# The first token tile in two halves, zero products on TensorE meanwhile, other banks for the first projections, and an earlier sum in the last stage

## The chip, the cores and the metric

The kernel runs on one core of a Trainium2 chip. The metric is the device time of one execution in microseconds (us), lower is better; the time before is the median of three runs. The engines are TensorE (PE, with its weight loads as PEld), VectorE (DVE), ScalarE (ACT), GpSimd (POOL) and SyncE (SP, which here only issues transfers). Each engine works through its own queue in order, and semaphores join the queues.

## What is computed

One decoder layer on 512 tokens of width 1024, with 16 learned meta tokens put ahead of them (so 528 positions). What matters here is the beginning and the end:

```python
h = jnp.concatenate([meta, x], axis=1)
mix = hybrid_mixer(rmsnorm(h, norm_mix_pre[l]), w_in[l], ...)   # proj = hn @ w_in, split into rq rk rv rg sq sk sv ga gb
h = h + rmsnorm(mix, norm_mix_post[l])
ff = swiglu(rmsnorm(h, norm_ffn_pre[l]), w_ffn_in[l], w_ffn_out[l])
h = h + rmsnorm(ff, norm_ffn_post[l])
return h[:, N_META:]
```

where `rmsnorm(x, g) = x * rsqrt(mean(x*x) + 1e-6) * g`. The first part of the mixer that the kernel computes is the stick-breaking attention: 16 heads of width 64 from the columns sq, sk, sv of `w_in`.

## The kernel before

All matrix products are made in three: each operand is split into a high part (rounded to the product's format, by ACT) and a low part (the rest, by DVE), and high×high, high×low and low×high are added up in one bank. The helper `split` (line 98) does this; its ACT half is line 99 and its DVE half line 96 (`lo_of`). So every weight and every activation passes ACT and DVE once before TensorE can use it.

The tile framework orders the instructions of each engine: it takes them by a simulated timeline, with program order as priority, and allots the buffers of each pool. An instruction marked `keep_in_program_order` stays behind what was traced before it on its engine.

**The first stage** (lines 701 to 763) prepares the tokens and the first attention operands:

- The gain vector `norm_mix_pre` is loaded as `grow` (8 x 128), turned by TensorE, copied to `gcol` by ACT, and spread over all partitions by eight transposes into `gps`, which takes a double bank of PSUM from `bank_a`.
- `xload(i)` loads token tile i (128 tokens x 1024, 512 KB) into a part of `ysb` that is free at this time; tile 4 is the 16 meta tokens.
- `innorm(i)` takes the sum of squares on ACT (line 719, with its output thrown into a double bank `junk`), scales it on DVE, takes the power -0.5 on POOL (`rstd_of`, lines 142 and 143), multiplies the tile with it and with `gps` on DVE (`hx`, two instructions of 512 columns, line 724), transposes it in eight steps on TensorE (line 93) and splits it into `hT` and `hL`.
- `Values(c)` is a block of 256 columns of sv: 1 MB of weights, loaded by `load_units` into one of two `raw` buffers and split into two units of four row blocks each; there are five buffers for units. `part((j,))` makes 24 products of 256 columns for token tile j in a bank of `bank_p` (two single banks), and its result is split into `vt`. `tail` does the same for the meta tokens, 16 products of 256 columns.
- `qk_work(work, 0)` adds the projections q and k of the first pair of heads to a work list, which is drained after all of `Values`: q is 24 products of 512 columns in a bank of `bank_p`, k is two times 24 products of 264 columns in one bank each. Each bank is emptied by ACT (lines 506 to 526) and DVE (line 96).

Then the eight pairs of heads follow. In each, TensorE's order is fixed by hand (`pinned[0]`): the pair's scores (in `bank_a`), transposes and value products alternate with the projections of the next pair (in `bank_p`). The first piece of pair 0 is a stretch of projection q of pair 1 with no score in it; then come the scores.

**The last stage** (lines 1252 to 1268) finishes the second FFN product by token tiles. For each half c of a tile's 1024 columns, ACT takes the sum of squares of the bank (line 1260) and DVE multiplies the bank with the gain (line 1261). Then DVE adds both sums (line 1263), POOL takes the power -0.5 (line 1264), DVE scales and adds the residual (line 1267) and SP stores each half.

Of the kernel before, what the change touches and what calls it, by code (L numbers as in the profile page):

```python
# [10 lines left out]
F32 = mybir.dt.float32  # L11
F32R = mybir.dt.float32r
# [4 lines left out]
P = 128  # L17
# [17 lines left out]
def hybrid_block(  # L35
# [65 lines left out]
            tc.keep_in_program_order(ins)  # L101
        lo_of(lo, src, hi)

    def load_units(src, kn, cn, views, wun=wun):

        raw = wraw.tile([P, kn, cn], F32, tag="raw", name="raw")
        nc.sync.dma_start(raw, src.rearrange("(k p) c -> p k c", p=P))
        res = []
        for ks, kl, cs, cl in views:
            wh = wun.tile([P, kl, cl], F32R, tag="wh", name="wh")  # L110
            wl = wun.tile([P, kl, cl], F32R, tag="wl", name="wl")
            split(wh, wl, raw[:, ks : ks + kl, cs : cs + cl])
            res.append((wh, wl))
        return res
# [293 lines left out]
    with tc.tile_pool(name="s2", bufs=2, side=RS, reuse_waits="tile") as s2:  # L408
# [28 lines left out]
        class Values:  # L437
# [2 lines left out]
            def __init__(self, c):  # L440
                self.c = c

            def load(self):
                c = self.c
                src = w_in[:, O_SV + 256 * c : O_SV + 256 * (c + 1)]
                self.vt = vts[c] = s2.tile([P, NT, 4, P], F32R, tag="vt", name="vt")
                self.units = load_units(src, KD, 256, [(0, 4, 0, 256), (4, 4, 0, 256)])

            def part(self, js):
                vt = self.vt  # L450
# [43 lines left out]
        qks = {}  # L494
        flat = lambda t: t.rearrange("p a b -> p (a b)")

        def qk_work(work, p):
            def q_load():
                return feat_units(w_in[:, O_SQ + P * p : O_SQ + P * (p + 1)])

            def q_steps(us):
                ps = bank_p()
                yield from feat_steps(ps, us[0], xtok, ltok)
                qa = s2.tile([P, T], F32R, tag="qa", name="qa", bufs=1)
                qb = s2.tile([P, T], F32R, tag="qb", name="qb")
                nc.scalar.activation(qa[0:64], ps[0:64], AF.Copy)
                nc.scalar.activation(qb[64:128], ps[64:128], AF.Copy)
                lo_of(qa[64:128], ps[0:64], qa[0:64])
                lo_of(qb[0:64], ps[64:128], qb[64:128])
                qks[p] = [(qa, qb)]  # L510

            def k_load():
                return feat_units(w_in[:, O_SK + P * p : O_SK + P * (p + 1)])

            def k_steps(us):
                ka = s2.tile([P, 2, 264], F32R, tag="ka", name="ka", bufs=1)
                kb = s2.tile([P, 2, 264], F32R, tag="kb", name="kb")
                kl1 = kl1s[p % 2]
                for i in range(2):
                    cs = slice(264 * i, 264 * (i + 1))  # L520
                    pk = bank_p()[:, :264]
                    yield from feat_steps(pk, us[0], lambda k: hT[:, k, cs], lambda k: hL[:, k, cs])
                    nc.scalar.activation(ka[0:64, i], pk[0:64], AF.Copy)
                    nc.scalar.activation(ka[64:128, i], pk[0:64], AF.Copy)
                    nc.scalar.activation(kb[64:128, i], pk[64:128], AF.Copy)
                    nc.scalar.activation(kb[0:64, i], pk[64:128], AF.Copy)
                    lo_of(kl0[0:64, i], pk[0:64], ka[0:64, i])
                    lo_of(kl1[64:128, i], pk[64:128], kb[64:128, i])
                qks[p] += [(flat(ka), flat(kb)), (flat(kl0), flat(kl1))]

            work.add(q_load, q_steps)
            work.add(k_load, k_steps)

# [169 lines left out]
        xts = [ysb[:, 2 * i : 2 * i + 2, :].rearrange("p a b -> p (a b)") for i in range(NT)]  # L703
        xts.append(xts[0])
        gps = bank_a()

        def xload(i):
            if i == NT:
                nc.sync.dma_start(xts[i][:NM], meta)
            else:  # L710
                nc.sync.dma_start(xts[i], x[i * P : (i + 1) * P, :])

        def innorm(i):
# [2 lines left out]
            xt = xts[i]  # L716
            junk = bank_a().rearrange("p a b -> p (a b)")
            ss = cst.tile([P, 1], F32, name=f"ss{i}")
            nc.scalar.activation(junk[:n], xt[:n], AF.Square, accum_out=ss[:n])
            rstd_of(ss[:n], ss[:n], 1e-6, 1.0 / D, n)  # L720
            for j in range(2):
                hx = s2.tile([P, 512], F32, tag="qb", name="hx")
                cs = slice(512 * j, 512 * (j + 1))
# [4 lines left out]
                ks = slice(4 * j, 4 * j + 4)  # L728
                split(hT[:, ks, c0 : c0 + n], hL[:, ks, c0 : c0 + n], pt[:, :, :n])

        nc.sync.dma_start(grow, g_mix_pre.rearrange("o (k p) -> (o k) p", p=P))
        xload(0)

        pg = bank_b()
        turned(pg[:, :KD], grow, ident[:KD, :KD])
        nc.scalar.activation(gcol, pg[:, :KD], AF.Copy)
        for k in range(KD):
            turned(gps[:, k // 4, (k % 4) * P : (k % 4 + 1) * P], gcol[:, k : k + 1].to_broadcast([P, P]), ident)
        vals = [Values(0), Values(1)]
        innorm(0)  # L740
        vals[0].load()
        xload(1)
        vals[1].load()
        innorm(1)
        for i in range(2, NT + 1):
            xload(i)
        work = Work()
        qk_work(work, 0)
        for j in range(NT):
            for v in vals:  # L750
                for _ in v.part((j,)):
# [462 lines left out]
    with tc.tile_pool(name="s8", bufs=2, side=RS, reuse_waits="tile") as s8:  # L1214
# [38 lines left out]
        for i in range(NT):  # L1253
            sc, fo = [col("sc0"), col("sc1")], s8.tile([P, D], F32, tag="fo", name="fo")
            for c in range(2):
# [2 lines left out]
                cs = slice(512 * c, 512 * (c + 1))  # L1258
                sq = s8.tile([P, 512], F32, tag="sq", name="sq")
                nc.scalar.activation(sq, banks[i][c], AF.Square, scale=D**-0.5, accum_out=sc[c])  # L1260
                nc.vector.tensor_tensor(fo[:, cs], banks[i][c], gfin[:, cs], op=ALU.mult)
            rs = col("rs")
            nc.vector.scalar_tensor_tensor(rs, sc[0], 1e-6, sc[1], op0=ALU.add, op1=ALU.add)
            nc.gpsimd.tensor_tensor(rs, rs, nhalf, op=ALU.pow)
            for c in range(2):
                cs = slice(512 * c, 512 * (c + 1))
                nc.vector.scalar_tensor_tensor(fo[:, cs], fo[:, cs], rs, h2[:, i, cs], op0=ALU.mult, op1=ALU.add)
# [44 lines left out]
```

## Time and profile before

| | |
|---|---|
| median of 3 runs | 1215.48 us (1213.07 to 1216.57) |
| the profiled execution's own time | 1216.2 us |
| its span, first to last instruction | 1214.1 us |
| mean granted clock of TensorE | 0.997 |
| PE busy | 1169.6 us, 96% of the span |
| PEld busy | 1061.5 us, 87% |
| DVE busy | 865.4 us, 71% |
| ACT busy | 534.0 us, 44% |
| POOL busy | 396.4 us, 33% |

The profiled execution is 0.7 us above the median, and 2.1 us of it lie outside the span. Matmuls are pipelined, so that a busy PE is not PE at its peak: the time from one start to the next tells more than the busy time. All times of rows are counted from the span's start.

### The profile page before, as it was taken

The numbers are of one execution on the slowest core, as the hardware profiler recorded it, in microseconds if no ns is written. First come the engines' busy times: TensorE is split into PE (matmuls) and PEld (weight loads), VectorE is DVE, ScalarE is ACT, GpSimd is POOL, SyncE is SP. The second block draws the span as 40 slices with busy tenths as digits, with TensorE's granted clock in tenths as the row PEclk, the third lists the DMA queues.
The fourth block names the chain that finished last, engine by engine and source line by source line (L and its number), as shares of the span: only waits on it lengthen the run. The fifth ranks groups of instructions, "written<-read, shape, count | busy, mean of one in ns | idle before, by whom it ended". The sixth has DMA issues, their size and how long they took to land.

```text
span 1214.1 us, 18932 instructions
## 1 busy us (share of the span) xinstructions
PE 1169.6 (96%) x7629; PEld 1061.5 (87%) x7629; DVE 865.4 (71%) x1138; ACT 534.0 (44%) x873; POOL 396.4 (33%) x450
## 2 busy tenths in 40 slices
PE   7999998989999999999999999999999999999997
PEld 6888888888789998998899899778999999998886
DVE  6488888888536785486678657776789998983333
ACT  5476666655414435343343424334354444443221
POOL 2026766655032330240323020000255666620000
PEclk9999999999999999999999999999999999999999
DMA  6321111214634214122321424424222333353211
GB/s 193 88 83 57 53 52 36 70 45 139 208 123 148 70 45 139 36 80 91 116 70 45 139 70 148 138 87 156 71 81 94 105 105 107 103 176 119 90 49 70
DMA packets 94503, 118.25 MB, mean 97 GB/s; under 512 B 2488, under 2 KB 71104, under 8 KB 94416
## 3 DMA queue, kind: packets, MB, share of 16 engines
q1 hardware_dynamic: 93984, 115.98, 29.3%
q8 instruction: 60, 0.98, 0.3%
q10 hardware_dynamic: 432, 1.07, 0.3%
q14 instruction: 27, 0.22, 0.1%
HBM read 109.96 MB, written 7.08 MB: 96 GB/s over the span
## 4 chain that ended last, share of the span: by engine, by line
PE 75%; DVE 12%; POOL 4%; ACT 3%; DMA 3%; issue 2%; SPq 0%; DVEq 0%; POOLq 0%; ACTq 0%
PE pp L90 31%; PE pb L90 20%; PE pa L90 18%; PE pc L90 4%; DVE wl L96 3%; DVE sm L620 3%; PE pb L93 2%; DVE sp L621 2%; ACT wh L99 1%; POOL mg L629 1%; DMA raw<-in_w_in_dram 1%; DMA ysb<-in_x_dram 1%; POOL raw L255 1%; DVE kl L96 1%; POOL st L255 1%
## 5 line engine op out<-in xcount | busy, mean ns | idle before, releaser
L96 DVE TENSOR_TENSOR wl<-raw,wh 128x1024 fp32r<-128x1024 f32 (+1 forms) x202 | 264.7, 1319 | 80.2 <-ACT wh L99 77.0
L99 ACT ACTIVATE wh<-raw 128x1024 fp32r<-128x1024 f32 (+1 forms) x202 | 201.2, 1007 | 254.8 <-PE pp L90 84.9
L90 PE MATMUL pp<-hT,wh 128*128 128x512 f32 (+2 forms) x308 | 109.1, 354 | 13.3 <-DVE qb L96 8.1
L90 PE MATMUL pp<-hL,wh 128*128 128x512 f32 (+2 forms) x308 | 104.0, 338 | 0.0
L90 PE MATMUL pp<-hT,wl 128*128 128x512 f32 (+2 forms) x308 | 103.9, 337 | 0.0
L255 POOL TENSOR_TENSOR st<-raw 128x512 f32<-128x512 f32 x28 | 44.8, 1620 | 164.8 <-DMA raw<-in_w_in_dram 164.8
L96 DVE TENSOR_TENSOR wl<-st,wh 128x1024 fp32r<-128x1024 f32 x54 | 83.1, 1542 | 12.9 <-ACT wh L99 12.8
L90 PE MATMUL pp<-qk,wh 128*128 128x512 f32 x256 | 83.1, 399 | 2.0 <-ACT qk L99 1.7
L90 PE MATMUL pp<-wh,hT 128*128 128x256 f32 (+1 forms) x240 | 75.5, 315 | 2.5 <-DVE kl L96 1.8
L90 PEld LDWEIGHTS pp<-hT,wh 128*128 128x128 f32 x308 | 58.7, 190 | 20.5 <-issue 9.4
L90 PE MATMUL pp<-wh,hL 128*128 128x256 f32 (+1 forms) x240 | 74.0, 308 | 0.8 <-DVE ss L142 0.8
L90 PE MATMUL pp<-wl,hT 128*128 128x256 f32 (+1 forms) x240 | 73.5, 306 | 0.0
L99 ACT ACTIVATE wh<-st 128x1024 fp32r<-128x1024 f32 x54 | 56.1, 1056 | 37.2 <-POOL st L255 19.4
L143 POOL TENSOR_TENSOR rs<-rs,nhalf 128x1 f32<-128x1 f32 x20 | 12.7, 634 | 170.7 <-DVE rs L142 170.7
L629 POOL CAST mg<-sp 128x16 fp32r<-128x16 f32 x64 | 30.2, 472 | 112.5 <-DVE sp L621 52.4
L90 PEld LDWEIGHTS pp<-hT,wl 128*128 128x128 f32 x308 | 58.6, 190 | 6.1
L90 PEld LDWEIGHTS pp<-hL,wh 128*128 128x128 f32 x308 | 58.8, 191 | 3.8
L90 PE MATMUL pa<-hL,wh 128*128 128x264 f32 (+1 forms) x192 | 61.6, 321 | 0.0
L90 PE MATMUL pa<-hT,wl 128*128 128x264 f32 (+1 forms) x192 | 61.6, 321 | 0.0
L90 PE MATMUL pa<-hT,wh 128*128 128x264 f32 (+1 forms) x192 | 61.6, 321 | 0.0
L620 DVE TENSOR_TENSOR_SCAN sm<-sm,mask 128x528 f32<-128x528 f32 (+1 forms) x64 | 59.7, 945 | 2.2 <-ACT sm L616 1.7
L90 PEld LDWEIGHTS pp<-qk,wh 128*128 128x128 f32 x256 | 47.6, 188 | 13.4 <-ACT qk L99 2.4
(333 smaller groups left out, 3825.6 us busy)
## 6 DMA issues: line engine op xcount, KB each, us to landing
raw<-in_w_in_dram SPq DMA_DIRECT2D x31, 1024.0 KB, 5.0
raw<-in_w_ffn_in_dram SPq DMA_DIRECT2D x22, 1024.0 KB, 5.2
raw<-in_w_in_dram SPq DMA_DIRECT2D x26, 512.0 KB, 4.1
raw<-in_w_ffn_out_dram SPq DMA_DIRECT2D x11, 1024.0 KB, 5.0
raw<-in_w_ret_out_dram SPq DMA_DIRECT2D x8, 1024.0 KB, 5.1
raw<-in_w_sb_out_dram SPq DMA_DIRECT2D x4, 1024.0 KB, 7.5
raw<-in_w_out_dram SPq DMA_DIRECT2D x4, 1024.0 KB, 5.1
ysb<-in_x_dram SPq DMA_DIRECT2D x4, 512.0 KB, 8.8
```

The lines of the kernel that those rows point to most:

```text
L90: return keep(nc.tensor.matmul(*args, **kw))
L93: return keep(nc.tensor.transpose(dst, src, idn))
L96: nc.vector.tensor_tensor(lo, src, hi.bitcast(F32), op=ALU.subtract)
L99: ins = nc.scalar.activation(hi, src, AF.Copy)
L143: nc.gpsimd.tensor_tensor(dst, dst, nhalf[:n], op=ALU.pow)
L255: nc.gpsimd.tensor_tensor(d[:, k : k + 2], p[:, k : k + 2], q[:, k : k + 2], op=op)
L620: nc.vector.tensor_tensor_scan(rev, rev, mask[:, r0:][:, ::-1], 0.0, op0=ALU.mult, op1=ALU.max)
L621: nc.vector.tensor_tensor(sp, sp, sm[:, r0 + 1 : L + 1], op=ALU.mult)
L629: nc.gpsimd.tensor_copy(g[:, i, 0:NM], att[i][:, 0:NM])
```

## The change

- Token tile 0 is loaded as two halves of 512 columns, one issued by SP, the other by ACT. The gain vector is issued by ACT too, behind that half, and no longer by SP ahead of the tile.
- The weights of `Values(0)` are loaded as two transfers of 512 KB, one for each unit, and its load is traced ahead of `innorm(0)`, as is `xload(1)`.
- The sum of squares of tile 0 is shared: ACT takes 512 columns, DVE the other 512 (into a buffer `jv`, of the tag that `hx` uses too), and a DVE instruction of one column adds them.
- TensorE makes 16 products of zeros (128 x 128 x 128) in a bank of `bank_p` before the gain vector is turned, and 6 more after the eight transposes of `gps`. They are kept in program order.
- q and k of pair 0 take the first half of a double bank of `bank_a`, not a bank of `bank_p`.
- In the last stage the sum and the power come ahead of the second multiplication with the gain.

```diff
-    def load_units(src, kn, cn, views, wun=wun):
+    def load_units(src, kn, cn, views, wun=wun, apart=False):
         raw = wraw.tile([P, kn, cn], F32, tag="raw", name="raw")
-        nc.sync.dma_start(raw, src.rearrange("(k p) c -> p k c", p=P))
+        rows = src.rearrange("(k p) c -> p k c", p=P)
+        if not apart:
+            nc.sync.dma_start(raw, rows)
         res = []
         for ks, kl, cs, cl in views:
+            if apart:
+                nc.sync.dma_start(raw[:, ks : ks + kl], rows[:, ks : ks + kl])
...
-        def qk_work(work, p):
+        def qk_work(work, p, bank=bank_p):
...
-                ps = bank_p()
+                ps = bank()
...
-                    pk = bank_p()[:, :264]
+                    pk = bank()[:, :264]
...
+        IDLE = (16, 6)
         def xload(i):
             if i == NT:
                 nc.sync.dma_start(xts[i][:NM], meta)
+            elif i == 0:
+                nc.sync.dma_start(xts[0][:, 0:512], x[0:P, 0:512])
+                nc.scalar.dma_start(xts[0][:, 512:D], x[0:P, 512:D])
...
-            nc.scalar.activation(junk[:n], xt[:n], AF.Square, accum_out=ss[:n])
-            rstd_of(ss[:n], ss[:n], 1e-6, 1.0 / D, n)
+            if i == 0:
+                so = cst.tile([P, 1], F32, name="so")
+                jv = s2.tile([P, 512], F32, tag="qb", name="jv")
+                nc.scalar.activation(junk[:, 0:512], xt[:, 0:512], AF.Square, scale=D**-0.5, accum_out=ss)
+                nc.vector.scalar_tensor_tensor(jv, xt[:, 512:D], 1.0 / D, xt[:, 512:D], op0=ALU.mult, op1=ALU.mult, accum_out=so)
+                nc.vector.scalar_tensor_tensor(ss, ss, 1e-6, so, op0=ALU.add, op1=ALU.add)
+                nc.gpsimd.tensor_tensor(ss, ss, nhalf, op=ALU.pow)
+            else:
+                nc.scalar.activation(junk[:n], xt[:n], AF.Square, accum_out=ss[:n])
+                rstd_of(ss[:n], ss[:n], 1e-6, 1.0 / D, n)
...
-        nc.sync.dma_start(grow, g_mix_pre.rearrange("o (k p) -> (o k) p", p=P))
         xload(0)
+        nc.scalar.dma_start(grow, g_mix_pre.rearrange("o (k p) -> (o k) p", p=P))
+        vals = [Values(0), Values(1)]
+        vals[0].load(apart=True)
+        xload(1)
+        zeros = s2.tile([P, P], F32R, tag="vs", name="zeros", bufs=1)
+        nc.vector.memset(zeros.bitcast(F32), 0.0)
+        idle = bank_p()
+        def idling(n):
+            for _ in range(n):
+                tc.keep_in_program_order(nc.tensor.matmul(idle[:, 0:P], zeros, zeros, start=True, stop=True))
+        idling(IDLE[0])
         pg = bank_b()
         turned(pg[:, :KD], grow, ident[:KD, :KD])
         nc.scalar.activation(gcol, pg[:, :KD], AF.Copy)
         for k in range(KD):
             turned(gps[:, k // 4, (k % 4) * P : (k % 4 + 1) * P], gcol[:, k : k + 1].to_broadcast([P, P]), ident)
-        vals = [Values(0), Values(1)]
+        idling(IDLE[1])
         innorm(0)
-        vals[0].load()
-        xload(1)
         vals[1].load()
...
-        qk_work(work, 0)
+        qk_work(work, 0, lambda: bank_a()[:, 0, :])
...
                 nc.scalar.activation(sq, banks[i][c], AF.Square, scale=D**-0.5, accum_out=sc[c])
+                if c:
+                    rs = col("rs")
+                    nc.vector.scalar_tensor_tensor(rs, sc[0], 1e-6, sc[1], op0=ALU.add, op1=ALU.add)
+                    nc.gpsimd.tensor_tensor(rs, rs, nhalf, op=ALU.pow)
                 nc.vector.tensor_tensor(fo[:, cs], banks[i][c], gfin[:, cs], op=ALU.mult)
-            rs = col("rs")
-            nc.vector.scalar_tensor_tensor(rs, sc[0], 1e-6, sc[1], op0=ALU.add, op1=ALU.add)
-            nc.gpsimd.tensor_tensor(rs, rs, nhalf, op=ALU.pow)
```

## Rows read from the trace of the kernel before

**Rows 1.** The chain of waits, 0 to 120 us: start, length, what.

```profile
5.55 10.20 DMA ysb<-in_x_dram
...
28.76 5.67 PE pp L90 x48
...
52.51 5.91 DMA raw<-in_w_in_dram
```

**Rows 2.** Busy time in stretches: stretch, length, then each engine, clock, DMA share, GB/s.

```profile
10.10:20.30 10.20, 8.88 (x58) 8.50 (x58) 9.44 (x16) 9.50 (x18) 2.17 (x4) 1.00 0.83 249
20.30:21.40 1.10, 0.14 (x3) 0.05 (x1) 1.10 (x3) 0.31 (x2) 0.00 (x0) 1.00 0.00 0
21.40:44.50 23.10, 23.10 (x198) 22.94 (x199) 11.16 (x26) 7.38 (x15) 0.00 (x0) 1.00 0.09 24
```

**Rows 3.** Timeline of SP's queue: start, length of the issue, instruction.

```profile
0.73 0.39 SPq L731 DMA_DIRECT2D grow<-in_norm_mix_pre_dram  x1
1.18 0.36 SPq L711 DMA_DIRECT2D ysb<-in_x_dram  x1
```

**Rows 4.** Busy time in half microseconds, the ramp of the transfers; last number GB/s.

```profile
2.00:2.50 0.50, 0.00 (x0) 0.00 (x0) 0.00 (x0) 0.01 (x1) 0.46 (x2) 1.00 0.94 115
2.50:3.00 0.50, 0.27 (x1) 0.18 (x1) 0.00 (x0) 0.00 (x0) 0.50 (x5) 1.00 0.77 229
...
4.50:5.00 0.50, 0.50 (x4) 0.32 (x2) 0.00 (x0) 0.00 (x0) 0.50 (x2) 1.00 1.08 383
```

**Rows 5.** Timeline of ACT, first stage; in brackets the idle time before it.

```profile
0.72 1.28 ACT L736 ACT_TABLE_LOAD   x1 [0.72 <-PEq L1298]
...
5.12 1.03 ACT L719 ACTIVATE pa<-ysb 128x1024 f32<-128x1024 f32 x1 [1.91 <-DMA ysb<-in_x_dram]
...
8.11 2.00 ACT L99 ACTIVATE wh<-raw 128x1024 fp32r<-128x1024 f32 x2 [1.85 <-DMA raw<-in_w_in_dram]
...
15.83 1.03 ACT L719 ACTIVATE pa<-ysb 128x1024 f32<-128x1024 f32 x1 [0.38 <-DMA ysb<-in_x_dram]
...
19.28 1.05 ACT L99 ACTIVATE hT<-pb 128x512 fp32r<-128x512 f32 x2
```

**Rows 6.** Timeline of DVE, first stage.

```profile
7.12 1.41 DVE L724 SCALAR_TENSOR_TENSOR hx<-ysb,ss,pa 128x512 f32<-128x512 f32 x2 [0.67 <-POOL ss L143]
```

**Rows 7.** Timeline of PE, first stage: gain, tile 0, two products of its first block.

```profile
2.72 0.27 PE L93 MATMUL pb<-ident,grow 8*128 8x8 f32 x1 [2.72 <-POOL ident masks.py:199]
...
3.26 1.97 PE L93 MATMUL pa<-ident,gcol 128*128 128x128 f32 x8 [0.27 <-ACT gcol L736]
...
7.93 1.97 PE L93 MATMUL pb<-ident,hx 128*128 128x128 f32 x8 [2.70 <-DVE hx L724]
...
13.02 0.41 PE L90 MATMUL pp<-wh,hL 128*128 128x256 f32 x1
...
13.24 0.41 PE L90 MATMUL pp<-wh,hT 128*128 128x256 f32 x1
```

**Rows 8.** Timeline of PE where pair 0 begins.

```profile
54.05 0.36 PE L90 MATMUL pp<-hT,wh 128*128 128x264 f32 x1 [0.85 <-DVE qb L96]
...
58.41 0.48 PE L90 MATMUL pp<-hT,wh 128*128 128x512 f32 x1 [1.21 <-DVE kl L96]
```

**Rows 9.** Timeline of ACT where pair 0 begins.

```profile
58.50 1.06 ACT L99 ACTIVATE wh<-raw 128x1024 fp32r<-128x1024 f32 x1 [1.14 <-DMA raw<-in_w_in_dram]
...
62.48 0.61 ACT L616 ACTIVATE sm<-pa 128x528 f32<-128x528 f32 x1
```

**Rows 10.** Timeline of all engines at the end.

```profile
1208.08 0.69 DVE L1261 TENSOR_TENSOR fo<-pc,gfin 128x512 f32<-128x512 f32 x1 [2.00 <-ACT sq L1260]
1208.69 0.15 DVE L1263 SCALAR_TENSOR_TENSOR rs<-sc,sc 128x1 f32<-128x1 f32 x1
1208.91 0.55 POOL L1264 TENSOR_TENSOR rs<-rs,nhalf 128x1 f32<-128x1 f32 x1 [4.89 <-DVE rs L1263]
1209.50 1.42 DVE L1267 SCALAR_TENSOR_TENSOR fo<-fo,rs,h 128x512 f32<-128x512 f32 x2 [0.66 <-POOL rs L1264]
```

More of the change, by code (lines that the diff above doesn't have):

```diff
@@ L441, in __init__, with load @@
                 self.c = c
-            def load(self):
+            def load(self, apart=False):
                 c = self.c
@@ L446, in load @@
                 self.vt = vts[c] = s2.tile([P, NT, 4, P], F32R, tag="vt", name="vt")
-                self.units = load_units(src, KD, 256, [(0, 4, 0, 256), (4, 4, 0, 256)])
+                self.units = load_units(src, KD, 256, [(0, 4, 0, 256), (4, 4, 0, 256)], apart=apart)
             def part(self, js):
```

## The prediction, made before the changed kernel was run

> **What bounds the kernel now.** The summary of busy times comes first: TensorE is busy 96% of the span, so only places where it waits, and the two ends of the span, can give anything. The change touches the first 60 us and the last 6, so I read those stages.
>
> In the chain of waits of the first 120 us one transfer stands out, that of a token tile, 10.2 us long and landing at 15.75 [rows 1]. ACT waits for it (0.38 us) and squares that tile, the fourth, at 15.83 [rows 5]. Then its queue holds the squares of the meta tile and a weight split, and only at 19.28 the high parts of tile 1 [rows 5]; DVE follows with the low parts, and TensorE, busy 0.14 of 1.10 us between 20.30 and 21.40, goes on when these have freed a bank. From there to 44.50 it is busy without a gap [rows 2]. So everything behind 21.4 us starts as early as the first stage lets it. In that stage, from 10.10 to 20.30, ACT is busy 9.50 of 10.20 us and DVE 9.44, TensorE 8.88 [rows 2]: two helpers and a transfer are the bound, and TensorE only follows.
>
> The start of the stage is looser. ACT waits 1.91 us for tile 0 and 1.85 us for the first megabyte of weights [rows 5], and DVE's first real work is the scaling of tile 0 at 7.12 [rows 6].
>
> TensorE runs slowly there. The granted clock stands at 1.00 in these rows [rows 2], yet products of 256 columns start 0.22 us apart at 13 us (256/0.22 is 1.2 GHz) and 0.118 apart later (48 in 5.67 us, the level of 2.4 GHz with a little on top) [rows 7, 1]. Ahead of the slow ones TensorE had only short bursts: the eight gain transposes from 3.26, the eight of tile 0 from 7.93 [rows 7].
>
> At the other end the order of the last tile is plain: the gain multiplication at 1208.08, the sum at 1208.69, the power at 1208.91, the scaling at 1209.50 [rows 10].
>
> **The change, part by part.**
>
> *The last stage.* ACT's sum releases DVE at 1208.08. Now the sum goes first, so the power starts 0.22 us after it (1208.91 - 1208.69), at 1208.30, and releases the scaling 0.59 us later (1209.50 - 1208.91), at 1208.89. The multiplication, 0.69 us, starts some 0.1 us behind the sum and is over at about the same time. The scaling moves from 1209.50 to 1208.89: **-0.6 us**, and the stores follow it. Bounds -0.5 and -0.65. The other three tiles have TensorE running beside them; nothing there counts.
>
> *Tile 0 on two queues, gain vector away from SP.* SP's first issue was the gain vector at 0.73, tile 0 came at 1.18 [rows 3]. So the whole stream of transfers on SP starts 0.45 us earlier. It is a stream at full rate: 115, then 229 GB/s in the first two half microseconds, 383 by 4.5 us [rows 4]. A second queue at the start could at best remove the ramp: (383-115) x 0.5 + (383-229) x 0.5 = 211 KB, 0.55 us at 383 GB/s. The bounds for the tile that lands at 15.75 are thus 0.45 and 1.0 us earlier. The Trainium skill speaks against the second queue ("DMA: Bandwidth & Descriptors", section "Issuing engines are not separate DMA queues"): transfers begun by different engines run on the same sixteen DMA engines, and only issue time is saved. By that rule this term would be 0.45 us; the trace of before has no second queue in this stage to say.
>
> *Half of the squares to DVE.* ACT took 1.03 us for 1024 columns, and takes about 0.53 for 512 (two splits of that size in 1.05 [rows 5]). DVE has nothing to do then, and its half costs 0.7 like an instruction of `hx` (1.41/2 [rows 6]), beside ACT's 0.53 and the reading of its sum: **0.4 us** earlier. With the 0.45 of the transfer, `hx` could start at 7.12 - 0.85 = 6.3.
>
> *The gain vector behind tile 0.* This works the other way. Before, turning it waited only for the identity matrix, at 2.72 [rows 7]. Now it lands with or behind tile 0, near 5.12 - 0.45 = 4.7. From turning it to the first spread took 0.54 us (3.26 - 2.72), and if ACT first does its squares 0.7 more; the eight transposes take 1.97, four of them 1.0. So the first half of `gps` is there at 6.2 to 6.9, the second at 7.2 to 7.9. Before, the second `hx` ran at about 7.8. What `hx` gains is therefore 0 to 0.85 us; I take 0.5.
>
> *The zero products.* 128 columns at the slow rate are 0.11 us: 16 take 1.8 us, where TensorE was idle to 2.72 anyway and now waits for the gain vector until 4.7. They cost nothing. The six take 0.65 us, between the eight gain transposes and those of tile 0, which were due at 7.93: from 7.2 to 7.9 they end at 7.85 to 8.55, so they may cost up to 0.6 us there. What they can give is the faster clock earlier: at most 24 products of the first block x (0.22 - 0.118) = 2.4 us, and about 1 us of the eight transposes. But TensorE is not the bound of this stage. As long as ACT's queue puts the high parts of tile 1 behind the squares of tile 3, a faster product waits longer. Between 0 and 2.4 us I take 0.3.
>
> *Weights in halves.* 512 KB less to wait for is 1.4 us at 383 GB/s, so the first split starts at about 8.11 - 1.4 - 0.45 = 6.3, in ACT's idle 1.85 us, and the two splits (2.00 us) end 1.4 us earlier or a little more. ACT and DVE, the full engines, get this lead. It is lost again at 15.75 - 0.45 to 1.0, where ACT waits for tile 3, unless ACT's queue is ordered anew. That the load is traced ahead of `innorm(0)` gives its splits the priority on ACT and DVE.
>
> *Sum of the first stage.* Lower end: the transfer alone, 0.45 us. Upper end with ACT's order as it is: 1.0 by the transfer, plus the 0.38 that ACT waited and some of the lead, 1.9. I take **-1.4**, nearer to the upper end, since both full engines are relieved.
>
> *Other banks for q and k of pair 0.* Two waits of TensorE stand there: 0.85 us at 54.05 and 1.21 at 58.41 [rows 8]. The first is k's second half waiting for q's bank; with two double banks it is the same rotation, and it stays. The second is pair 1's q waiting for a bank of k; now both `bank_p` are free, and it goes: 1.2 us. But what comes next is late for another reason. ACT waits until 58.50 for a weight transfer that was under way from 52.51 for 5.91 us [rows 1, 9], then splits it, empties k, loads a function table and makes the first sigmoid at 62.48 [rows 9]. No score is used before. So TensorE's wait moves behind pair 1's q: I take **0**; without that cover it is -1.2. The scores now share double banks with q and k, which can cost about 0.2.
>
> Sum: 0.6 + 1.4 + 0 = 2.0 us. Against the profiled execution's own 1216.2 that gives 1214.2; that execution lies 0.7 above the median, so the forecast is 1215.48 - 2.0 = **1213.5 us**, 0.16% less. A measurement of this kernel can tell about 0.3% from no change, 3.6 us: faster means below 1211.8, slower above 1219.1.
>
> **The rivals.**
>
> *The first stage is ordered anew and TensorE becomes its bound.* The whole gain then shows. From 9.9, where tile 0's transposes ended [rows 7], to 44.5 us TensorE has to make 192 + 32 products of 256 columns at 0.118 (26.4 us), about 3 us of transposes of the other tiles, and waits at least 0.5 for tile 0's split: 29.9 of 34.6 us. So 4.7 us are there, and the 0.5 of an earlier `hx`. For it: ACT and DVE get a lead of 1.4 us, and the fast clock brings tile 1's transposes forward. Against it: they were full for 10 us, and the order of ACT put tile 1 behind tile 3. If most of it comes, 3 to 4.5 us, with 0.6 at the end and up to 1.2 at pair 0: 4 to 6 us, **1209.5 to 1211.5**.
>
> *Only the end gains.* The gain vector's lateness and the six zero products use up what tile 0 wins, and ACT's lead is lost at tile 3's transfer: -0.6 to -1, **1214.7**. For it: 7.2 to 7.9 against 7.8 above.
>
> *Slower: tile 0's second half is late.* ACT's first instruction was a table load, 0.72 to 2.00 [rows 5]. If it stays first, the half is issued 0.8 us later than the tile was, behind 512 KB of weights on SP: landing at 5.12 + 0.8 + up to 1.4 = 5.9 to 7.3, the gain vector behind it, its eight transposes (2.5 us with what leads to them) by 8.4 to 9.8. `hx` is then 0.6 to 2 us later than at 7.8, and with 0.6 back at the end the kernel is 0 to 1.4 us slower, **1216** in the middle. It decides from an issue after 1.6 us on. The Trainium skill ("ScalarE: Activation LUTs", section "Step-by-step: what each stage is for") says that the compiler places a table load right before the ACTIVATE that needs it; by that the two issues would go first. That lowers this chance. To be slower by over 0.3% the new order of ACT and DVE would have to lose another 2 us: splits of weights put ahead of `hx` in DVE's queue, 1.2 us each (their priority rose), are the only row that could.
>
> **How the numbers follow.** The forecast 0.47, the new order 0.31, only the end 0.14, slower than before 0.08. Faster by over 0.3%: the new order, and a few of the forecast's upper cases, 0.33. Slower by over 0.3%: most of the order that loses is within it, 0.07 with what I cannot see in a framework that orders the whole program again. Within: 0.60. The forecast alone reaches from 1212.3 to 1214.9. The range for 8 in 10 takes in most of the new order below and the slower case above: 1209.5 to 1216.8.
>
> **What would show it.** Right: tile 0 squared before 4.8 us, tile 3's transfer landing at about 15, TensorE without a gap from about 20 instead of 21.4, its wait near 58 gone but the first sigmoid earlier only by what the first stage gave; at the end the sum ahead of the multiplication, 0.6 us from there. The new order would show as TensorE without a gap from 17 to 18 us, and tile 1's high parts ahead of tile 3's squares. The forecast is wrong if products of 256 columns are still 0.22 apart behind 13 us and nothing else moved, if ACT loads its table before it issues, or if the time comes from behind 65 us, where nothing was changed but the order could be.

## The result and the profile after

The changed kernel takes 1217.37 us (median of 16 runs), the kernel before 1215.62 us beside it: ratio 1.0014 (95% interval 1.0008 to 1.0021; intervals stand in brackets from here on). The forecast was 1213.5 us. So the kernel became slower, by 1.75 us; that is less than the 0.3% set as a bound, but the interval excludes a gain. The time lies above the range too. The profiled execution took 1217.72 us, its span 1215.4 us.

The stage that was to gain, in the three stretches of [rows 2]:

```profile
10.10:20.30 10.20, 7.29 (x33) 6.44 (x33) 9.02 (x16) 7.96 (x14) 1.88 (x4) 1.00 0.77 244
20.30:21.40 1.10, 1.10 (x7) 1.10 (x7) 0.30 (x1) 0.00 (x0) 0.28 (x1) 1.00 0.16 40
21.40:44.50 23.10, 23.10 (x195) 22.89 (x194) 10.40 (x25) 5.87 (x14) 0.00 (x0) 1.00 0.08 23
```

TensorE's gap at 20.3 to 21.4 us is gone, as forecast. But in the 10.2 us ahead of it TensorE made 33 instructions, not 58, and ACT was busy 7.96 us, not 9.50. Less was done by the full engines, not more. ACT's timeline, which answers to [rows 5], says why:

```profile
0.73 0.39 ACTq L717 DMA_DIRECT2D ysb<-in_x_dram  x1
1.15 0.58 ACTq L749 DMA_DIRECT2D grow<-in_norm_mix_pre_dram  x1
1.76 1.28 ACT L99 ACT_TABLE_LOAD   x1 [1.76 <-issue]
6.43 1.06 ACT L99 ACTIVATE wh<-raw 128x1024 fp32r<-128x1024 f32 x1 [3.38 <-DMA raw<-in_w_in_dram]
7.39 0.16 ACT L766 ACTIVATE gcol<-pb 128x8 f32<-128x8 f32 x1
...
12.22 2.00 ACT L99 ACTIVATE wh<-raw 128x1024 fp32r<-128x1024 f32 x2 [1.79 <-DMA raw<-in_w_in_dram]
14.13 1.07 ACT L99 ACTIVATE hT<-pb 128x512 fp32r<-128x512 f32 x2
```

Read it from the bottom. Tile 0's high parts (`hT`) run at 14.13 us. They stand behind the two splits of the second block of weights, `Values(1)`, and these waited 1.79 us at the head of the queue for their transfer. In the kernel before it was the other way round: its `hT` ran at 10.02 and 11.54 us and these splits at 12.40:

```profile
10.02 0.58 ACT L99 ACTIVATE hT<-pb 128x512 fp32r<-128x512 f32 x1
...
12.40 2.00 ACT L99 ACTIVATE wh<-raw 128x1024 fp32r<-128x1024 f32 x2 [0.28 <-DMA raw<-in_w_in_dram]
```

Further up, the copy of the gain (`gcol`) stands behind a split of weights, at 7.39 us instead of 3.02. DVE has taken the same order:

```profile
7.52 1.23 DVE L96 TENSOR_TENSOR wl<-raw,wh 128x1024 fp32r<-128x1024 f32 x1 [1.81 <-ACT wh L99]
...
9.14 1.23 DVE L96 TENSOR_TENSOR wl<-raw,wh 128x1024 fp32r<-128x1024 f32 x1 [0.33 <-ACT wh L99]
10.28 1.40 DVE L741 SCALAR_TENSOR_TENSOR hx<-ysb,ss,pa 128x512 f32<-128x512 f32 x2
...
13.75 2.35 DVE L96 TENSOR_TENSOR wl<-raw,wh 128x1024 fp32r<-128x1024 f32 x2
16.02 1.28 DVE L96 TENSOR_TENSOR hL<-pb,hT 128x512 fp32r<-128x512 f32 x2
```

Two things are late here, and the experiments have to part them: `hx` at 10.28 us (7.12 in [rows 6]), and the low parts `hL` at 16.02, behind the splits of `Values(1)`. The first of them in the kernel before:

```profile
11.48 0.68 DVE L96 TENSOR_TENSOR hL<-pb,hT 128x512 fp32r<-128x512 f32 x1
```

TensorE, to compare with [rows 7]:

```profile
1.08 3.68 PE L760 MATMUL pp<-zeros 128*128 128x128 f32 x16 [1.08 <-DVE zeros L755]
5.33 0.24 PE L93 MATMUL pb<-ident,grow 8*128 8x8 f32 x1 [0.57 <-DMA grow<-in_norm_mix_pre_dram]
7.61 1.97 PE L93 MATMUL pa<-ident,gcol 128*128 128x128 f32 x8 [2.04 <-ACT gcol L766]
...
11.08 1.97 PE L93 MATMUL pb<-ident,hx 128*128 128x128 f32 x8 [0.33 <-DVE hx L741]
14.76 0.58 PE L90 MATMUL pp<-wh,hT 128*128 128x256 f32 x1 [1.71 <-ACT hT L99]
...
22.36 0.28 PE L90 MATMUL pp<-wh,hT 128*128 128x256 f32 x1
22.48 0.28 PE L90 MATMUL pp<-wl,hT 128*128 128x256 f32 x1
```

The first product of the first block starts at 14.76 us. Its products start 0.21 us apart until 22.36 us and 0.12 apart from there. In the kernel before the first product and that change came at:

```profile
10.65 0.58 PE L90 MATMUL pp<-wh,hT 128*128 128x256 f32 x1 [0.76 <-ACT hT L99]
...
15.35 0.28 PE L90 MATMUL pp<-wl,hT 128*128 128x256 f32 x1
```

The delay, 4.1 us at the first product, has grown to 6.3 us at the 24th (22.48 against 16.18). At the first sigmoid, [rows 9], 3.6 us of it are left, 66.07 us instead of 62.48:

```profile
66.07 0.61 ACT L620 ACTIVATE sm<-pa 128x528 f32<-128x528 f32 x1
```

From some 72 us on the instruction orders of the two kernels are alike, and the lag stays at 3.6 to 4.5 us up to 480 us; some of it is absorbed in waits for transfers later (3.1 at 840, 2.1 at 1142 us). At the end, [rows 10], the forecast 0.6 us come:

```profile
1210.17 0.16 DVE L1291 SCALAR_TENSOR_TENSOR rs<-sc,sc 128x1 f32<-128x1 f32 x1 [2.03 <-ACT sq L1288]
1210.25 0.68 DVE L1293 TENSOR_TENSOR fo<-pc,gfin 128x512 f32<-128x512 f32 x1
...
1210.99 1.41 DVE L1296 SCALAR_TENSOR_TENSOR fo<-fo,rs,h 128x512 f32<-128x512 f32 x2
```

From ACT's sum to the scaling it takes 0.82 us (1210.99 - 1210.17), before 1.42 (1209.50 - 1208.08).

### The profile page after: what moved, and what is told of

It is laid out like the page before. It is cut to its first block, busy times and chain, and to the rows that moved or that the text cites. A ratio compares the mean times of both kernels' runs of the same rounds, so it can differ in the third digit from the quotient of the medians.

```text
span 1215.4 us, 18984 instructions
## 1 busy us (share of the span) xinstructions
PE 1174.6 (97%) x7651; PEld 1067.5 (88%) x7651; DVE 868.5 (71%) x1141; ACT 533.8 (44%) x873; POOL 393.5 (32%) x450
## 3 DMA queue, kind: packets, MB, share of 16 engines
q10 hardware_dynamic: 592, 1.33, 0.3%
## 4 chain that ended last, share of the span: by engine, by line
PE 73%; DVE 12%; POOL 4%; issue 3%; ACT 3%; DMA 3%; DVEq 0%; POOLq 0%; SPq 0%; ACTq 0%
PE pp L90 31%; PE pb L90 18%; PE pa L90 17%; PE pc L90 4%; DVE wl L96 4%; DVE sm L624 3%; PE pb L93 3%; DMA raw<-in_w_in_dram 2%; ACT wh L99 2%; DVE sp L625 2%; POOL mg L633 1%; POOL raw L259 1%; POOL st L259 1%; DMA raw<-in_w_sb_out_dram 1%; POOL mg L634 1%
## 5 line engine op out<-in xcount | busy, mean ns | idle before, releaser
L90 PE MATMUL pp<-hT,wh 128*128 128x512 f32 (+2 forms) x284 | 101.3, 357 | 11.1 <-DVE qb L96 7.1
L90 PE MATMUL pp<-hT,wl 128*128 128x512 f32 (+2 forms) x284 | 96.2, 339 | 0.0
L90 PE MATMUL pp<-hL,wh 128*128 128x512 f32 (+2 forms) x284 | 96.0, 338 | 0.0
L90 PE MATMUL pa<-hT,wh 128*128 128x264 f32 (+1 forms) x216 | 69.4, 321 | 1.3 <-DVE qb L96 1.3
L90 PEld LDWEIGHTS pp<-hT,wh 128*128 128x128 f32 x284 | 54.1, 191 | 17.6 <-issue 7.8
L90 PE MATMUL pa<-hL,wh 128*128 128x264 f32 (+1 forms) x216 | 69.4, 321 | 0.0
L90 PE MATMUL pa<-hT,wl 128*128 128x264 f32 (+1 forms) x216 | 69.3, 321 | 0.0
L90 PEld LDWEIGHTS pp<-hT,wl 128*128 128x128 f32 x284 | 53.9, 190 | 5.8
L90 PEld LDWEIGHTS pp<-hL,wh 128*128 128x128 f32 x284 | 54.2, 191 | 3.5
```

The lines of the kernel that those rows point to most:

```text
L90: return keep(nc.tensor.matmul(*args, **kw))
```

## The experiments

The kernel before, measured beside each, had medians of 1215.62 to 1215.82 us. The first sigmoid is that of one profiled execution, and scatters: in e3, whose start is that of the kernel before, it came 0.6 us later. Nor does it order the medians: e7 has the earliest first sigmoid, e6 the lowest median.

| run | what it is | first sigmoid | median | ratio to before |
|---|---|---|---|---|
| after | the change | 66.07 | 1217.37 | 1.0014 [1.0008, 1.0021] |
| e1 | after, gain vector first on SP | 62.77 | 1213.45 | 0.9981 [0.9973, 0.9990] |
| e2 | after, first splits behind tile 0's squares | 62.19 | 1212.96 | 0.9976 [0.9966, 0.9986] |
| e3 | before + the end | 63.08 | 1215.04 | 1.0000 [0.9991, 1.0008] |
| e4 | before + the banks | 63.12 | 1215.55 | 0.9999 [0.9990, 1.0007] |
| e5 | after without zero products | 65.06 | 1219.06 | 1.0026 [1.0015, 1.0037] |
| e6 | after, second splits behind tile 0 | 61.52 | 1212.65 | 0.9973 [0.9962, 0.9985] |
| e7 | e1 without zero products | 59.73 | 1213.07 | 0.9978 [0.9967, 0.9989] |
| e8 | before, gain vector on ACT's queue | 62.37 | 1215.65 | 0.9998 [0.9989, 1.0007] |
| e9 | before + tile 0 in halves | 64.73 | 1215.90 | 1.0000 [0.9992, 1.0009] |
| e10 | e7, weights in one transfer | 62.73 | 1215.36 | 0.9997 [0.9988, 1.0005] |
| e11 | e7, 17 zero products in the gaps | 60.49 | 1213.94 | 0.9979 [0.9969, 0.9989] |
| e12 | before + weights in halves | 61.48 | 1214.83 | 0.9993 [0.9984, 1.0001] |
| e13 | e12 + the end | 61.39 | 1213.81 | 0.9987 [0.9978, 0.9996] |

**e1, the gain vector back at the head of SP's queue.**

```diff
-        xload(0)
-        nc.scalar.dma_start(grow, ...)
+        nc.sync.dma_start(grow, ...)
+        xload(0)
```

> The changed kernel with one edit: the gain vector is issued by SP ahead of tile 0 again, as before the change. Theory (ACT's order): the gain vector on ACT's queue comes late, and with it the scheduler puts the split of the first weights ahead of the copy of the gain and the squares of tile 0; with the gain first, the squares should start near 5 us instead of 7.45, the scaling of tile 0 near 6.5 to 7 instead of 10.28, the first sigmoid at 62.5 or earlier instead of 66.07, and the time should be 1213 to 1215 us, 0.9982 to 0.9997 of before. Rival (zero products): they still hold TensorE to 4.8 us and between the gain and tile 0; first sigmoid at 65 or later, ratio 1.001. Rival (banks of q and k): the loss lies behind 44 us and stays; ratio 1.001.

One line makes the slower kernel a faster one. ACT's and DVE's timelines of this run:

```profile
12.22 0.60 ACT L99 ACTIVATE hT<-pb 128x512 fp32r<-128x512 f32 x1
...
13.96 2.01 ACT L99 ACTIVATE wh<-raw 128x1024 fp32r<-128x1024 f32 x2 [0.28 <-DMA raw<-in_w_in_dram]
```

```profile
10.27 1.40 DVE L741 SCALAR_TENSOR_TENSOR hx<-ysb,ss,pa 128x512 f32<-128x512 f32 x2
```

`hx` is as late as in the changed kernel (10.27 against 10.28 us, for the first low part of the weights still stands ahead of it), and yet the first sigmoid is 3.3 us earlier. What is different is that `hT` stands ahead of the splits of `Values(1)`. So the late `hx` is not the price. (It is late against the theory too, which had it at 6.5 to 7 us.)

**e2, the order by hand.** The first pair's load is traced inside `innorm(0)`, between the squares and `hx`, with its splits kept in program order on ACT; the gain vector stays where the change put it.

```diff
-        vals[0].load(apart=True)
-        xload(1)
...
+        def load_first():
+            split_in_order[0] = True
+            vals[0].load(apart=True)
+            split_in_order[0] = False
+            xload(1)
...
-        innorm(0)
+        innorm(0, load_first)
```

> The changed kernel with transfers and queues as they are, and only ACT's order set by hand: the first weight splits are kept behind the squares of tile 0. Theory (ACT's order): copy of the gain and squares at about 5.7 to 6.5 us; DVE still has one weight split ahead of the scaling of tile 0, which starts at 8 to 9 us instead of 10.28; first sigmoid 1 to 2 us earlier than the 66.07 of the changed kernel; ratio to before 1.0000, between 0.9992 and 1.0008. If the gain vector's late landing at 5.3 us is the cost by itself, and not the order behind it, the first sigmoid stays at 65.5 or later and the ratio at 1.001.

Here too tile 0's first high part (11.35 us) stands ahead of the second splits (12.95). The late landing of the gain vector alone does not cost the time. The gain is larger than this run's theory had it (first sigmoid at 64 to 65 us, ratio 0.9992 to 1.0008); the edit to the first splits has moved the second splits too.

**e6, only the second splits put back.** This settles it: everything of the change is kept, the first splits and the late `hx` too, and only the splits of `Values(1)` are held behind tile 0.

```diff
         innorm(0)
+        split_in_order[0] = True
         vals[1].load()
+        split_in_order[0] = False
```

> The changed kernel with one thing kept by hand: the splits of the second pair of weights stand behind tile 0's high and low parts. The gain vector, the first splits, the squares and the late hx (10.3 us) stay. Theory (that order is the price): first product at 12 to 13 us, fast clock by 16, first sigmoid 62.2 to 63.2 us instead of 66.1, ratio to the kernel before 0.9975 to 0.9995. Rival (the late hx and the late gain vector are the price, and the order only follows them): first sigmoid 65 us or later, ratio 1.0005 to 1.0020.

DVE, ACT and TensorE of this run:

```profile
10.24 1.40 DVE L741 SCALAR_TENSOR_TENSOR hx<-ysb,ss,pa 128x512 f32<-128x512 f32 x2
...
13.03 0.69 DVE L96 TENSOR_TENSOR hL<-pb,hT 128x512 fp32r<-128x512 f32 x1
```

```profile
12.19 0.60 ACT L99 ACTIVATE hT<-pb 128x512 fp32r<-128x512 f32 x1 [1.83 <-PE pb L93]
...
13.54 2.00 ACT L99 ACTIVATE wh<-raw 128x1024 fp32r<-128x1024 f32 x2
...
61.52 0.61 ACT L620 ACTIVATE sm<-pa 128x528 f32<-128x528 f32 x1
```

```profile
12.84 0.58 PE L90 MATMUL pp<-wh,hT 128*128 128x256 f32 x1
...
15.17 0.28 PE L90 MATMUL pp<-wl,hT 128*128 128x256 f32 x1
...
17.86 0.28 PE L90 MATMUL pp<-wl,hT 128*128 128x256 f32 x1
```

With `hx` at 10.24 us the first product starts 1.9 us earlier than in the changed kernel and the first sigmoid 4.55; the ratio goes from 1.0014 to 0.9973, 5.0 us (0.0041 x 1215.8). Both are somewhat better than this run's theory had them.

The two traces also tell what the order costs. It is not the wait for the transfer. In e6 ACT waits for tile 0's transposes until 12.19 us, and in the changed kernel these start only 0.04 us later (11.08 against 11.04); so ACT had nothing of tile 0 to do before the transfer was there at 12.2. Tile 0 stands behind the work of the splits, 2.00 us on ACT (first product 1.9 us later) and 2.35 on DVE (`hL` 3.0 us later).

The rest of the 4.55 us comes up behind the first product: up to the 24th TensorE takes 7.72 us in the changed kernel and 5.02 in e6. Of this difference of 2.7 us 0.64 is a longer wait for `hL` (0.87 against 0.23); most of the rest is the spacing, 0.21 us up to 22.36 in the one and 0.12 from 15.17 on in the other. In e6 the products follow tile 0's transposes at once; in the changed kernel TensorE stood idle for 1.71 us before them. How much of it the order has to answer for is not shown: these are single executions, and in e5 below, with the changed kernel's order on ACT, the same stretch took 6.47 us.

**e3 and e4, the end and the banks alone**, each put into the kernel before as in the diff of the change.

> The kernel before with the sum and the power ahead of the second gain multiplication in the last stage, and nothing else. From the last tile's sum of squares on ACT to its scaling 0.6 us less; ratio 0.9995. If the power or the stores behind it were held by something else, 1.0000.

> The kernel before with q and k of pair 0 in double banks, and nothing else. Theory (ACT's order): TensorE's wait of 1.2 us near 58 us goes, the first sigmoid stays at 62.5 within 0.3, ratio 1.0000. Rival (banks): the scores wait for the shared double banks, first sigmoid 1.5 to 3.5 us later, ratio 1.001 to 1.003. Forecast's other end: the wait that goes is gained, ratio 0.999.

Neither moves the time by what can be resolved. In the trace of e3 the scaling starts 0.82 us behind the sum, at 1208.47, so the 0.6 us are there. With the banks, TensorE's wait at 58.41 of [rows 8] is gone from the trace of the changed kernel as well, and the one for q's bank stays (1.33 us there); the first sigmoid waits for ACT, as forecast. In e4 itself it came at 63.12 us, 0.3 outside the theory; there as in e3 the transfers at the start landed 0.4 to 0.5 us later than in the trace of the kernel before.

**e5, e7 and e11, the zero products.** e5 sets both counts to 0 in the changed kernel, e7 does so in e1.

```diff
-        idling(IDLE[0])
+        idling(0)
...
-        idling(IDLE[1])
+        idling(0)
```

> The changed kernel without its 22 zero products; ACT's order is unchanged by it. In the changed kernel the 16 end before the gain vector is there (5.3 us) and the six end at 10.8, ahead of the transposes of hx at 11.1, which wait for DVE. Theory (the changed kernel loses because the splits of the second pair of weights stand ahead of tile 0's high and low parts on ACT and DVE): nothing changes, first product still at 14 to 15 us, first sigmoid 65.5 to 66.5 us, ratio to the kernel before 1.0005 to 1.0022. Rival (the zero products hold TensorE's transposes back or cost the clock): first product by 13 us, fast clock by 16, ratio 0.9985 to 1.0000.

> The changed kernel with the gain vector back at the head of SP's queue and without the 22 zero products; DVE then takes hx ahead of the first low part of the weights. With the zero products this kernel measured 0.9981 [0.9973, 0.9990] of the kernel before. Theory (the zero products give nothing that lasts; the early hx moves the first product up by about 1.5 us, and the first sigmoid follows ACT): hx before 8 us, first product at 11 to 11.5, first sigmoid 62.0 to 62.8, ratio 0.9970 to 0.9985. Rival (the zero products are what brought that kernel the fast clock early): fast clock later than 16 us, first sigmoid 63 or later, ratio 0.9990 to 1.0005.

Without them the changed kernel gains nothing: in e5 ACT's order is unchanged (second splits at 12.55 us, `hT` at 14.46, first product at 15.09), and the ratio is a little above the theory's numbers. It is even 0.0012 (1.5 us) above that with them, but the intervals overlap. e1 loses nothing without them (e7). In e7 `hx` runs at 5.83 us, the first product at 9.60 and the first sigmoid at 59.73, the last two earlier than forecast, and the ratio is as forecast: not all of an early start reaches the end. In e1 the zero products did two things that cancel as far as the times tell: they held TensorE, so that the gain vector was turned at 4.68 us and not at 2.72 (e7), and the spacing of 0.12 us came 2.6 us behind the first product and not 5.1. e11 then puts them where TensorE is idle, by hand in its order: 7, 6 and 4.

```diff
-        IDLE = (16, 6)
+        IDLE = (7, 6, 4)
...
+        pinned[0] = True
         idling(IDLE[0])
...
-        innorm(0)
+        innorm(0, lambda: idling(IDLE[2]))
+        pinned[0] = False
```

> The same kernel (gain vector at the head of SP's queue) with 17 zero products put where TensorE stands idle, by hand in its order: 7 ahead of the gain vector's transpose, 6 behind the gain products, 4 behind tile 0's transposes. If the zero products can bring the fast clock forward: products 0.12 us apart from 11 to 12 us instead of 14.6, first sigmoid 57.9 to 59.2 us, ratio to the kernel before 0.9960 to 0.9975. If they give nothing that lasts: fast clock from 13.5 us or later, first sigmoid 59.4 to 60.5 us, ratio 0.9970 to 0.9988.

TensorE in e11:

```profile
1.08 1.76 PE L762 MATMUL pp<-zeros 128*128 128x128 f32 x7 [1.08 <-DVE zeros L757]
...
4.93 1.52 PE L762 MATMUL pp<-zeros 128*128 128x128 f32 x6
...
8.27 1.09 PE L762 MATMUL pp<-zeros 128*128 128x128 f32 x4
10.64 0.58 PE L90 MATMUL pp<-wh,hT 128*128 128x256 f32 x1 [1.28 <-ACT hT L99]
...
15.76 0.28 PE L90 MATMUL pp<-wl,hT 128*128 128x256 f32 x1
```

The products come 0.12 us apart from 15.76 us, in e7, without any zero product, from 14.73. The first product was 1.0 us later here, behind weights that landed later; counted from it, the change comes after 5.1 us in both. The zero products bring nothing forward: 0.9979 against 0.9978.

**e8, the gain vector alone moved to ACT's queue**, in the kernel before.

```diff
-        nc.sync.dma_start(grow, ...)
         xload(0)
+        nc.scalar.dma_start(grow, ...)
```

> The kernel before with one line moved: ACT issues the gain vector behind tile 0, which SP issues whole and now first. ACT's order becomes gain column, square of tile 0, both first splits, square of tile 1, tile 0's two high parts, the second splits: the gain is late, but the second splits stay behind tile 0. Theory (the late gain alone costs little where the order of the second splits stays): first sigmoid 62.3 to 63.5 us, ratio 0.9995 to 1.0010. Rival (a late gain vector costs by itself what the changed kernel loses): first sigmoid 65 us or later, ratio 1.0015 to 1.0030.

This was no test of a late gain vector: with nothing ahead of it on that queue it was issued at 0.72 us, and `gcol` ran at 3.03 as before. It shows that the queue alone costs nothing; in the changed kernel the half tile stands ahead of it. ACT took the square of tile 1 ahead of `hT`, so the first product came at 11.80 us, 1.15 later than before, and yet the first sigmoid at 62.37.

**e9 and e10, tile 0 in halves, and the weights whole again.** e9 is the kernel before with the halves of tile 0 and of its squares; e10 is e7 with the halves of the weights undone.

```diff
+            elif i == 0:
+                nc.sync.dma_start(xts[0][:, 0:512], x[0:P, 0:512])
+                nc.scalar.dma_start(xts[0][:, 512:D], x[0:P, 512:D])
```

```diff
-        vals[0].load(apart=True)
+        vals[0].load()
```

> The kernel before with one part of the change alone: tile 0 fetched in halves on SP's and ACT's queues and squared in halves by ACT and DVE, the gain vector first on SP's queue as before. Theory (this part gives what the prediction gave it, and no order changes): hx at 6.0 to 6.6 us instead of 7.1, first sigmoid 0.4 to 1.2 us earlier than the 62.5 of the kernel before, ratio 0.9985 to 0.9998. Rival (the whole 2.7 us by which the best kernel so far has its first sigmoid earlier come from here): first sigmoid by 60.3 us, ratio 0.9970 to 0.9985.

> The kernel with the gain vector at the head of SP's queue and without zero products (0.9978 [0.9967, 0.9989], first sigmoid 59.7 us), with one thing undone: the first pair's weights come as one transfer again. Theory (the halves give about what their lead on ACT is worth): the first two splits together behind 7.9 us instead of 6.6 and 8.0, first product 0.5 to 1.0 us later than 9.6, first sigmoid 60.2 to 61.0 us, ratio to the kernel before 0.9975 to 0.9990. Rival (the halves give nothing, ACT waits for the second half anyway): first sigmoid within 0.3 us of 59.7, ratio as without the edit.

In e9 `hx` runs at 5.81 us, 1.3 us earlier, and it is worth nothing by the median. The trace shows what ACT waits for next:

```profile
9.81 2.00 ACT L99 ACTIVATE wh<-raw 128x1024 fp32r<-128x1024 f32 x2 [4.92 <-DMA raw<-in_w_in_dram]
11.71 0.58 ACT L99 ACTIVATE hT<-pb 128x512 fp32r<-128x512 f32 x1
```

Tile 0's high part stands behind the split of the first megabyte of weights, and ACT waits 4.92 us for that. The weights came 1.7 us later here than in [rows 5]; the first sigmoid, 64.73, fits neither theory, and the median shows no loss. That may be no accident: of the five traces with the gain vector first on SP and tile 0 on both queues (e1, e7, e9, e10, e11) only e7 has the whole first megabyte at 8.0 us, the others at 9.0 to 9.8; with tile 0 whole (the kernel before, e3, e4, e8, e12, e13) it was there at 7.9 to 8.6. Whether the halves are worth nothing because ACT waits for the weights anyway, or because they delay these, e9 does not part. In e10, without the halves of the weights, e7's 0.9978 becomes 0.9997, not to be told from the kernel before, and the first sigmoid moves to 62.73. That is more than the theory had given them (60.2 to 61.0, 0.9975 to 0.9990).

**e12 and e13, the weights in halves alone, and with the end.** The diff of `load_units` and `vals[0].load(apart=True)` of the change, in the kernel before.

> The kernel before with one part of the change alone: the first pair's weights as two transfers on SP's queue, each with its split behind it. Theory (this part carries the gain that the repaired versions show, since ACT and TensorE wait for these weights and not for tile 0): first split 1.0 to 1.7 us earlier than the 8.1 of the kernel before, first product 0.5 to 1.2 us earlier than 10.65, first sigmoid 60.5 to 62.0 us, ratio 0.9975 to 0.9993. Rival (ACT waits for the second half anyway, and the parts pay only together): first product within 0.4 us of 10.65, first sigmoid 62.2 to 63.0 us, ratio 0.9993 to 1.0008.

> The kernel before with the weights in two transfers and the sum first at the end, and nothing else of the change. By the theory that these two parts are what gains: the time of the former run less 0.6 us, ratio 0.9970 to 0.9988, as good as the four repaired versions of the changed kernel (0.9973 to 0.9981). By the rival (the parts pay only together): ratio 0.9990 to 1.0003.

ACT in e12:

```profile
6.51 1.06 ACT L99 ACTIVATE wh<-raw 128x1024 fp32r<-128x1024 f32 x1 [0.37 <-DMA raw<-in_w_in_dram]
```

The first split is 1.6 us earlier than in [rows 5], the first product 1.05 (9.60 against 10.65), the first sigmoid 1.0. The ratio, 0.9993 [0.9984, 1.0001], is that of a gain of 0.85 us, at the edge of what the measurement tells. With the end it is 0.9987, a gain that the interval holds up.

The best of all is e6 (0.9973), but the intervals of e1, e2, e6, e7 and e11 overlap. Any of them beats both kernels.

## Why the prediction was wrong, point by point

*The step that failed* is the sum of the first stage, put at -1.4 us on the ground that "both full engines are relieved". It took ACT's and DVE's order as given, except in two rivals. Its inputs failed less than its frame: in the changed kernel the scheduler put the splits of `Values(1)` ahead of tile 0's high and low parts, 2.00 us of work on ACT at the moment when tile 0 was ready for it, and 2.35 us on DVE. In the trace this stage came out at +3.6 us, by the first sigmoid. With that one order put back (e6) the kernel measured 1212.65 us, 5.0 us less, and the other repaired versions 1212.96 to 1213.94. That these lie beside the forecast, 1213.5, is luck. The sum rested on the transfer of tile 3 and took only some of the lead of the weights. In the changed kernel that transfer did come as forecast, at 14.8 us, 0.9 earlier, and it did not help: ACT, behind the second splits, came to the square only at 16.26. In e1 it came at 16.7 us, 0.9 later than before, and the kernel gained. What carries most of the gain is the weights, see below.

TensorE was without a gap from 16.85 us, earlier than the sign given for the order that gains (17 to 18), with a loss: the sign does not tell how much is done by then.

*The gain vector behind tile 0* brought the new order: with its load back at the head of SP's queue, tile 0 stands ahead of the second splits again (e1). It was priced by leaving `hx` a gain of 0 to 0.85 us, with the first half of `gps` at 6.2 to 6.9 us. The vector was turned at 5.33 us, not 4.7, and then `gcol` stood behind a split of weights on ACT: `gps` began at 7.61. The text named the splits in front as a possible loss, but as a direct one of 1.2 us each in front of `hx`. Those splits did come, and e6, which keeps both, shows that they cost little; the loss came from the next pair of splits. That the load was traced ahead of `innorm(0)` did not do it by itself: e1 keeps that and has tile 0 ahead of the second splits.

*Tile 0 on two queues* and *half of the squares* moved `hx` as forecast or by more (5.81 us in e9, where 6.3 was worked out), and are worth nothing by themselves (1.0000). [Rows 5] give one reason: the wait of 1.85 us for the weights stood behind the squares, and ahead of tile 0's high parts. That the weights came later beside them, as above, may be another. The transfers themselves gave no more bytes for the second queue, see below.

*Weights in halves* was called a lead that is lost again at tile 3. As far as the runs tell, it carries most of the gain: 0.85 us alone (e12, not clear of nothing), 2.3 us between e10 and e7 (0.0019 x 1215.8, the two intervals just touch). Whether it gains more beside an early tile 0 than alone is not resolved.

*Zero products*: taken as 0.3 us of gain; none was measured in e1 against e7, and in the changed kernel (e5) a gain of some 1.5 us is neither shown nor excluded. They were mis-sized too: the 16 take 3.68 us, 0.23 each, where 0.11 was estimated. They end at 4.76 us, before the gain vector is there at 5.3, and so cost nothing in the changed kernel.

*Other banks* (0) and *the last stage* (-0.6) are right by their traces; alone, neither can be told from nothing in time.

*The rivals.* That ACT loads its table first did not happen: both issues went at 0.73 and 1.15 us and the load at 1.76. The Trainium skill ("ScalarE: Activation LUTs", section "Step-by-step: what each stage is for") says that the compiler puts a table load right before the ACTIVATE that needs it; the trace agrees. A slower kernel was given 0.08 by way of that late half, and an order that loses over 0.3% 0.07 with all that was unseen. Nobody can read a scheduler's answer from a trace of before, but that a late operand changes an order, and that the order decides what stands ahead of ready work, deserved a rival of its own.

## What to carry to other kernels

Where a framework orders each engine's queue, an edit that delays one small operand can reorder the large instructions around it; compare the orders of the two programs in the stage of the change before pricing any term. A late instruction cost little by itself here; what cost was ready work that stood behind other work on both helper engines, and the slow spacing of TensorE behind that. And relieve what the engine waits for last: here, as far as the runs tell, the first megabyte of weights, not the token tile.

## What the runs showed of the hardware

A second queue moved no more bytes at the start. In the first 12 us, the kernel before and e9, from the view of the transfers (packets, MB, share of 16 engines; then KB each, median us from issue to landing):

```profile
q1 hardware_dynamic: 2466, 3.49, 86.4%
...
raw<-in_w_in_dram SPq DMA_DIRECT2D x2, 1024.0 KB, 8.1
```

```profile
q1 hardware_dynamic: 2381, 3.17, 74.8%
q10 hardware_dynamic: 144, 0.26, 7.6%
...
raw<-in_w_in_dram SPq DMA_DIRECT2D x2, 1024.0 KB, 9.9
ysb<-in_x_dram ACTq DMA_DIRECT2D x1, 256.0 KB, 2.8
```

3.43 MB on two queues against 3.49 on one: the halves of tile 0 came early, and the weights later. In the changed kernel, whose halves are issued together at 0.73 us, it was 3.55. The Trainium skill ("DMA: Bandwidth & Descriptors", section "Issuing engines are not separate DMA queues") says that transfers begun by different engines share the same sixteen engines; the trace agrees.

Near 74 us, where TensorE had waited much, the granted clock was 0.50 in the profiled executions of some kernels and 1.00 in others with nearly the same work ahead, the kernel before and e2:

```profile
70.00:74.00 4.00, 1.50 (x8) 1.31 (x9) 3.89 (x7) 1.65 (x6) 1.13 (x4) 0.92 0.45 131
74.00:76.00 2.00, 2.00 (x11) 2.00 (x10) 1.97 (x5) 1.04 (x3) 0.88 (x2) 0.50 0.00 0
```

```profile
70.00:74.00 4.00, 1.62 (x11) 1.44 (x12) 3.92 (x6) 1.96 (x7) 1.10 (x4) 1.00 0.47 131
74.00:76.00 2.00, 2.00 (x19) 2.00 (x18) 1.97 (x5) 0.90 (x4) 1.01 (x3) 1.00 0.00 0
```

0.50 is the level of 1.2 GHz. From 70 to 96 us e2 gained 1.7 us on the kernel before, with the same order of instructions. Nor is it the program alone: e3, the kernel before but for the last stage, had 1.00 there, with 1.66 us busy ahead. The spacing at the start scatters in the same way: 0.12 us from 15.35 us on in the kernel before, from about 18 on in e3. What decides it stays open; it is one reason why single executions of this kernel scatter by a microsecond or two.
